# A two-layer trunk on one core: loads in layer 0's planner, column sums of the end in one group, paired stores, and a new order of layer 1's tiles

## The chip, the cores and the metric

The program runs on one NeuronCore of one Trainium2 chip. The metric is the device time of one execution in microseconds (us), the median over several runs. The profile is one execution of its own, recorded by the hardware profiler. Five engines work beside each other, each through its own queue in order: TensorE (PE, matrix products), VectorE (DVE), ScalarE (ACT), GpSimd (POOL) and SyncE (SP, which here only issues transfers).

## The reference

One step of a network with two layers on 640 tokens (128 of a prompt, 512 on a grid 64 columns wide) of 1024 features, all in f32. Cut to what matters:

```python
for i in range(2):                      # layer 0: conv branch, layer 1: SSD branch
    sh, sc, gt = split(silu(cond) @ ada_w[i] + ada_b[i], 3)
    h = rms_norm(y, norm_g[i]) * (1 + sc) + sh
    if i == 0:
        a, a_gate, z = split(h @ w_in + b_in, 3)               # 2048 features each
        v = depthwise_conv(a * sigmoid(a_gate), w_dw, b_dw)    # 31 taps, inside a grid row
        out = (silu(layer_norm(v)) * silu(z)) @ w_out
    else:
        z, xbc, dt_raw = split(h @ w_in)                       # 2048, 3072, 64
        xs, B, C = split(silu(depthwise_conv(xbc, w_conv, b_conv)))   # 5 taps
        dt = softplus(dt_raw + bias)                           # forward and backward
        yf = ssd_scan(xs, dt_f, B, C); yb = reversed ssd_scan  # chunks of 128 tokens
        out = rms_norm((yf + yb + d * xs) * silu(z)) @ w_out   # norm in 4 groups
    y = y + gt * out
return rms_norm(y, final_norm_g), final states
```

Prompt and grid have their own conditioning vectors and their own gate, scale and shift.

## The kernel before

**Layout.** Features lie on the 128 partitions, tokens along the row. The residual x is 8 tiles of 128 features x 640 tokens, the hidden width of 2048 is 16 tiles. The 640 tokens make two halves of 320 (`HN`), which fill the two banks of a PSUM tile.

**Products.** Each f32 product is made of three reduced-precision ones: a weight is split into a high part wh and a low part wl, the data into h_hi and h_lo, and wh·h_hi, wh·h_lo and wl·h_hi add up in PSUM. A projection of one 128-feature tile is 2 halves x 8 k-tiles x 3 = 48 matmuls of 320 columns (L619 in layer 0, `product`; L1277 in layer 1). For each weight tile, SP loads wf (L399), ScalarE casts wh (L418) and copies its negative to wl (L428), and GpSimd then issues a transfer of the same weights that adds onto wl (L429). In some steps of layer 0 and most of layer 1, VectorE subtracts instead (L1243). The tile wf has two buffers, wh and wl three.

**Layer 0.** For tile i, `a` and `g` are projected; ScalarE makes the sigmoid of g (L646), VectorE the product v (L659). The 31 taps on v are shared out: VectorE does most as multiply-adds in its own sum cva (L804); the widest-displaced `NPOOL[i]` taps are multiplied on ScalarE (tile tp, three buffers, L835) and added on GpSimd to cv (L876). VectorE's sum starts from a first term that ScalarE makes (L796), and is copied to cv by ScalarE (L811). Row crossings are put right in `seam_sums` (L848 to L870). `z` is projected and passed through silu (L675, which needs a table load on ScalarE), and the statistics of the layer norm come from column sums on TensorE, in the idle half of a bank, added up by VectorE (ssum, L730). The PSUM ring mm has two tiles: a projection can start when its tile's last reader is done. The modulation products of the coming steps ride on the same banks: `blocks` loads wa, four transfers of 256 KB for a block (L112), TensorE multiplies them ahead of a projection (L639), ScalarE copies the row (ada_row, L630), and TensorE turns it (L130), after which VectorE reads the values (L137).

**Layer 1.** 16 tiles x, 4 B, 4 C, 16 z, and 12 half-groups o of the output product are projected in an order written out by hand (names such as x21 are group and tile). The convolution of five taps on a projection is VectorE's (L1321) after ScalarE brings it out of PSUM (up, L1308). The time-step chain is a row of small steps on VectorE (L1867, L1870), whose results t, v, e and u TensorE turns to tokens (pt, L1934). The scan goes over groups and chunks: decays (L1618), chunk states pst (L1496) into VectorE's stn (L1524), from that po (L1559) and yo (L1563), then products py (L1627), gate and norm.

**The end.** The last output product (L1787) runs half 1 first, then half 0. Each of eight tiles gets its residual on VectorE (L1756), its square on ScalarE (L1761); GpSimd adds up the squares of the middle tiles. Column sums over the features are matmuls with ones (L184): a first group of two tiles of squares, copied to sm by VectorE (L1802), and a second group of the last tile, added to it (L1808). Then ScalarE's square root (L1809), the reciprocal (L1810) and a spread over the partitions on TensorE (L189). VectorE scales five tiles of a half straight from PSUM (L1815), GpSimd three from a copy of ScalarE's (L1823, L1826), and 16 stores of 128x320 leave from SP and ScalarE (L1830).

**The order of the work** is settled when the program is built. `Order` keeps a clock for each engine. Each chain of steps is a generator that yields operations with an engine and an estimated duration (`op`), keys to wait for (`key`) and buffers to take (`get`). `run` picks the operation that can start first, by the clocks, then by the priorities in PRIO0 and PRIO1 (lower first), and issues it. The emitted order is then fixed on every engine (`keep_order`), so planned durations and priorities decide the order and nothing else; at run time each engine waits at the head of its queue. PLAN0 and PLAN1 name the order in which weights are loaded and tiles projected. In `blocks` (L688) a block waits for the block two before it, and the first two have no condition. Transfers take only the clock of the engine that issues them.

Of the kernel before, what the change touches and what calls it, by code (L numbers as in the profile page):

```python
# [13 lines left out]
P = 128  # L14
# [35 lines left out]
def trunk(ctx: ExitStack, tc: tile.TileContext, a: dict):  # L50
# [193 lines left out]
    class Order:  # L244
# [63 lines left out]
        def run(self, until=None):  # L308
            while self.chains:
# [4 lines left out]
                for ch in self.chains:  # L314
# [3 lines left out]
                    for n, (eng, dur, fn, table) in enumerate(ways):  # L318
# [4 lines left out]
                        load = 1.28 if table and table != self.table else 0.0  # L323
# [6 lines left out]
                if table:  # L330
                    self.table = table
# [4 lines left out]
                ch[1] = t + dur + LATE.get(eng, 0.0)  # L336
                ch[5] = eng
# [6 lines left out]
    def op(eng, dur, fn, table=None):  # L344
        return "op", ((eng, dur, fn, table),)
# [4 lines left out]
    def key(*ks):  # L350
        return ("key",) + ks
# [26 lines left out]
    if True:  # L378
# [12 lines left out]
        def weights():  # L391
# [4 lines left out]
            for name, w in src:  # L396
                yield get("wf")
                wf = gp.tile([P, 1024], F32, tag="wf", bufs=2, name="wf")
                t = yield op(SP, 0.35, lambda: nc.sync.dma_start(out=wf, in_=w))  # L399
                start(split(name, wf, w), t)  # L400
# [186 lines left out]
    with tc.tile_pool(name="l0", bufs=1) as lp:  # L587
# [100 lines left out]
        def blocks():  # L688
            for n, (l, b) in enumerate(BLOCKS):
                if n > 1:  # L690
                    yield key(("ada", n - 2))
# [3 lines left out]
                t = yield op(SP, 1.8, lambda: blk.append(ada_load(l, b, cs, 2)))  # L695
# [146 lines left out]
        def seam_sums(i):  # L842
# [30 lines left out]
            for n, tap in enumerate(TAPS[:NPOOL[i]]):  # L873
                d, lo, hi = span_of(tap)
                yield key(("tp", i, n))
                t = yield op(PO, 1.28 + 0.0175 * (hi - lo - 49), lambda: G.tensor_add(out=rows64(cv[i], lo, hi), in0=rows64(cv[i], lo, hi), in1=sgs["tp", i, n][:, :, 0 : hi - lo]))  # L876
# [295 lines left out]
    if True:  # L1172
# [291 lines left out]
        def group(g):  # L1464
            yield key(("B", g), ("x", g, 3), *([("cols",)] if g == 0 else []))
# [286 lines left out]
        def last_residual(b, m, ps, ring):  # L1752
            tok = slice(b * HN, b * HN + HN)
            for cd, sl in SEGS:
                xv = x[m][:, tok][:, sl]
                t = yield op(VE, vec(sl.stop - sl.start) + 0.08, lambda: V.scalar_tensor_tensor(out=xv, in0=ps[:, sl], scalar=gain(1, m, cd), in1=xv, op0=ALU.mult, op1=ALU.add))  # L1756
            put(ring, t)
            nm, bufs = SQ[b]
            yield get(nm)
            sq = lp.tile([P, 512], F32, tag=nm, bufs=bufs, name="sq")[:, 0:HN] if b == 0 else lp.tile([P, HN], F32, tag=nm, bufs=bufs, name="sq")  # L1760
# [7 lines left out]
            post(("acc", b, m), t)  # L1768
            if m >= KD - REST[b]:
                t = yield op(ACT, 0.56, lambda: S.activation(out=x[m][:, tok], in_=x[m][:, tok], func=AF.Copy, scale=c("fg", m)))  # L1770
                post(("scaled", b, m), t)

        def last_products(b):
# [16 lines left out]
            post(("products", b), t)  # L1790

# [3 lines left out]
        def final(b):  # L1795
            tok = slice(b * HN, b * HN + HN)
            yield key(("acc", b, KD - 3), ("acc", b, KD - 2))
            yield get("b")
            ps = pq.tile([P, 512], F32, tag="b", bufs=3, name="rps")
            yield op(PE, 0.84, lambda: column_sums(ps[:, 384:387], accs[b][:2], PARTS))  # L1800
            sm, rc = (gp.tile([P, 3], F32, tag=nm, bufs=1, name=nm) for nm in ("sm", "rc"))
            yield op(VE, 0.16, lambda: V.tensor_copy(out=sm, in_=ps[:, 384:387]))  # L1802
# [314 lines left out]
```

## Time and profile before

| | us |
|---|---|
| median of 3 runs | 1088.61 (1088.28 to 1089.37) |
| profiled execution, its own time | 1088.08 |
| its span, first to last instruction | 1086.3 |
| TensorE busy | 1047.8 (96%) |
| VectorE, ScalarE, GpSimd busy | 795.1, 666.3, 456.4 |
| mean granted TensorE clock | 0.989 of full |

A row of the waits has the engine, the waiting operation with its line, what it waited for with its line, and the total, the count and the longest in us. A row of a timeline has the start, the duration from the first to the last of a row of like instructions, the engine, the line, the operation, output <- inputs, sizes and count; in brackets the idle time of the engine just before and what ended it. TensorE works through a pipeline: a matmul of 320 columns lasts about 0.31 us in a row, while the next starts 0.15 us after it. Numbers behind tile names are the program's own.

By place, TensorE's idle time in the span lies ahead of the first product and behind the last one (7.2 us at the start, 10.6 from the last product on), at a few places between, and hardly at all from 604 to 1070 us.

### The profile page before, as it was taken

How to read it: one execution, taken by the hardware profiler on the slowest of the kernel's cores; microseconds unless marked ns; L12 is line 12 of the kernel's file. 1: busy time of each engine (PE TensorE's matmuls, PEld its weight loads, DVE VectorE, ACT ScalarE, POOL GpSimd, SP SyncE). 2: the span in 40 equal slices, each digit the busy share in tenths (PEclk: the TensorE clock that was granted, in tenths of full speed). 3: DMA queues.
4: the chain of work that ended last, by engine and by line, in shares of the span. 5: the costliest groups of instructions: out<-in, count | busy, mean ns of one | idle time of the engine just before them, and what ended most of it. 6: DMA issues, size and time to landing. Idle time of an engine off the chain costs nothing. (4 is left out here: it accounts for less than half of the span.)

```text
span 1086.3 us, 19905 instructions
## 1 busy us (share of the span) xinstructions
PE 1047.8 (96%) x7888; PEld 976.3 (90%) x7888; DVE 795.1 (73%) x1188; ACT 666.3 (61%) x1093; POOL 456.4 (42%) x461
## 2 busy tenths in 40 slices
PE   6999999989999999999998999999999999999996
PEld 3898999989999999999998998988889988988895
DVE  2579999987999695103789597789777766776763
ACT  6457778878688686333576566585658353754442
POOL 0028989988599211111000145323531463364323
PEclk9999999999999999999999999999999999999997
DMA  9487787777755666676111635233341335343102
GB/s 362 181 227 190 205 214 180 183 206 209 189 124 135 138 144 152 150 163 130 59 63 66 160 87 136 69 108 98 107 117 64 102 107 127 91 105 107 40 20 97
DMA packets 86541, 146.94 MB, mean 135 GB/s; under 512 B 26928, under 2 KB 49840, under 8 KB 86448
## 3 DMA queue, kind: packets, MB, share of 16 engines
q1 hardware_dynamic: 77088, 113.91, 33.8%
q0 software_dynamic: 8640, 30.94, 16.3%
q8 instruction: 62, 1.02, 0.4%
q10 hardware_dynamic: 720, 0.82, 0.2%
q14 instruction: 31, 0.25, 0.1%
HBM read 140.73 MB, written 4.92 MB: 134 GB/s over the span
## 5 line engine op out<-in xcount | busy, mean ns | idle before, releaser
L804 DVE SCALAR_TENSOR_TENSOR cva<-v,cst,cva 128x620 f32<-128x620 f32 (+10 forms) x343 | 266.8, 823 | 16.3 <-ACT cva L796 11.8
L876 POOL TENSOR_TENSOR cv<-cv,tp 128x490 f32<-128x490 f32 (+5 forms) x137 | 174.9, 1276 | 10.1 <-ACT tp L835 1.2
L835 ACT ACTIVATE tp<-v,cst 128x490 f32<-128x490 f32 (+5 forms) x137 | 94.8, 719 | 41.6 <-POOL cv L876 41.2
L418 ACT CAST wh<-wf 128x1024 fp32r<-128x1024 f32 x63 | 65.9, 1045 | 67.9 <-PE o__5278 L155 29.9
L1239 ACT CAST wh<-wf 128x1024 fp32r<-128x1024 f32 x53 | 55.4, 1044 | 67.4 <-PE o L1277 25.6
L1277 PE MATMUL o<-yhl,wh 128*128 128x320 f32 x384 | 92.5, 328 | 0.0
L1277 PE MATMUL pz<-h_hi,wh 128*128 128x320 f32 x256 | 88.3, 345 | 1.3 <-ACT up L1308 1.3
L1243 DVE TENSOR_TENSOR wl<-wf,wh 128x1024 fp32r<-128x1024 f32 x48 | 66.2, 1379 | 31.5 <-ACT wh L1239 31.3
L1565 POOL TENSOR_TENSOR y<-y,yo 128x512 f32<-128x512 f32 x32 | 45.4, 1417 | 85.9 <-DVE yo L1563 82.6
L1277 PE MATMUL pz<-h_hi,wl 128*128 128x320 f32 x256 | 79.1, 309 | 0.0
L1277 PE MATMUL pz<-h_lo,wh 128*128 128x320 f32 x256 | 79.0, 309 | 0.0
L1277 PE MATMUL xs<-h_hi,wh 128*128 128x320 f32 x224 | 75.1, 335 | 0.0
L1321 DVE SCALAR_TENSOR_TENSOR xs<-up,cst,xs 128x642 f32<-128x642 f32 x64 | 66.1, 1032 | 7.4 <-PE ptx L1345 3.4
L1277 PEld LDWEIGHTS o<-yhl,wh 128*128 128x128 f32 x384 | 63.8, 188 | 7.5 <-issue 7.2
L1277 PE MATMUL xs<-h_lo,wh 128*128 128x320 f32 x224 | 69.9, 312 | 0.0
L1277 PE MATMUL xs<-h_hi,wl 128*128 128x320 f32 x224 | 69.9, 312 | 0.0
L429 POOL DMA_DIRECT2D wl<-w_in x43 | 37.4, 870 | 60.0 <-ACT wl L428 59.3
L428 ACT ACTIVATE wl<-wh 128x1024 fp32r<-128x1024 f32 x58 | 61.5, 1060 | 1.8
L1277 PE MATMUL o<-yhl,wl 128*128 128x320 f32 x192 | 59.4, 309 | 0.0
L1440 ACT ACTIVATE gf<-gf,cols 128x128 f32<-128x128 f32 x160 | 50.5, 391 | 8.5 <-DVE gf L1436 7.3
L1277 PEld LDWEIGHTS pz<-h_hi,wh 128*128 128x128 f32 x256 | 48.1, 188 | 7.2 <-issue 5.6
L1277 PEld LDWEIGHTS pz<-h_lo,wh 128*128 128x128 f32 x256 | 48.2, 188 | 3.8 <-issue 3.8
(842 smaller groups left out, 3379.3 us busy)
## 6 DMA issues: line engine op xcount, KB each, us to landing
wf<-w_in SPq DMA_DIRECT2D x48, 512.0 KB, 3.7
wl<-w_in POOLq DMA_DIRECT2D x43, 512.0 KB, 6.9
wa<-w_ada SPq DMA_DIRECT2D x64, 256.0 KB, 6.1
wf<-w_out SPq DMA_DIRECT2D x32, 512.0 KB, 3.7
wf<-w_xbc SPq DMA_DIRECT2D x24, 512.0 KB, 3.9
gf<-acd SPq DMA_DIRECT2D x40, 256.0 KB, 4.5
wa<-w_ada SPq DMA_DIRECT2D x16, 512.0 KB, 10.2
wf<-w_z SPq DMA_DIRECT2D x16, 512.0 KB, 3.7
```

What stands on the lines that cost most here:

```text
L418: t = yield op(ACT, 1.05, lambda: S.copy(out=wh, in_=wf))
L428: yield op(ACT, 1.06, lambda: S.activation(out=wl, in_=wh.bitcast(F32), func=AF.Copy, scale=-1.0))
L429: t = yield op(PD, 0.7, lambda: G.dma_start(out=wl, in_=src, accum_op=ALU.add))
L804: t = yield op(VE, 0.24 + 0.01 * (hi - lo), lambda: V.scalar_tensor_tensor(out=rows64(accs[i], lo, hi), in0=rows64(vs[i], lo + d, hi + d), ...
L835: t = yield op(ACT, 0.72, lambda: S.activation(out=tp[:, :, 0 : hi - lo], in_=rows64(vs[i], lo + d, hi + d), func=AF.Copy, scale=w_dw(i, t ...
L876: t = yield op(PO, 1.28 + 0.0175 * (hi - lo - 49), lambda: G.tensor_add(out=rows64(cv[i], lo, hi), in0=rows64(cv[i], lo, hi), in1=sgs["tp" ...
L1239: S.copy(out=cell["wh"], in_=cell["wf"])
L1243: e_.tensor_sub(out=cell["wl"], in0=cell["wf"], in1=cell["wh"].bitcast(F32))
L1277: T.matmul(ps[:, b, at_ : at_ + t1 - t0], lhsT=w_, rhs=t_[:, t0:t1], start=k == 0 and n == 0, stop=k == nk - 1 and n == 2)
L1321: t = yield op(VL, 0.89, lambda: V.scalar_tensor_tensor(out=acc, in0=u[:, d : d + PW], scalar=c("w_c", j * 5 + d), in1=acc, op0=ALU.mult, ...
L1440: t = yield op(ACT, 0.39, lambda: S.activation(out=gv[:, h_, :], in_=gv[:, h_, :], func=AF.Exp, bias=cols1[ch][:, o8 + h_ : o8 + h_ + 1]), ...
L1565: t = yield op(PO, 1.29, lambda: G.tensor_add(out=y, in0=y, in1=yo))
```

## The change

- `weights` and `blocks` in layer 0's planner: a load of SP or an adding load of GpSimd now moves a clock of the transfers (1.55 us for a wf, 3.1 for a block of wa or for an adding load), and its result is expected by that clock. The first two blocks wait for a weight's split; the rest as before. Some of GpSimd's and other estimates rise.
- PRIO0, PLAN0 and NPOOL: tiles 5 and 7 have 11 and 10 taps on GpSimd where they had 12; projection a15 stands behind z5 and z6.
- PRIO1 and PLAN1: every priority but a few, and the tile order of layer 1, are other numbers and another list. `group` waits for all four x tiles.
- The end: a group of column sums opens with a matmul of zeros (nil), adds nine matmuls in one PSUM group, and the square root reads PSUM; sm, its copy and its add are gone. The last tile's square of half 0 is made in two parts, the large one on ScalarE and the small one on VectorE. After half 1's products the planner's margin for TensorE is 0.3.
- x is one tile of 8 x 640 with views, and a store takes two feature tiles: 8 of 128x2x320.

The diff, cut to its core; of the two tile orders a part of a line stands here, and the priorities are left out:

```diff
-PLAN0 = "... g13 a13 g14 z4 a14 g15 a15 z5 z6 z7 ..."
-NPOOL = (12, 6, 12, 6, 12, 12, 8, 12, 2, 8, 9, 8, 12, 4, 6, 8)
+PLAN0 = "... g13 a13 g14 z4 a14 g15 z5 z6 a15 z7 ..."
+NPOOL = (12, 6, 12, 6, 12, 11, 8, 10, 2, 8, 9, 8, 12, 4, 6, 8)
...
-PLAN1 = "z00 x21 x03 b0 c0 x02 z01 x13 b1 x10 x11 z02 x12 z03 x20 ..."
+PLAN1 = "x03 z00 z01 x11 x02 b0 x10 c0 x13 z02 x31 c1 x21 x12 x20 ..."
...
-    x = []
-    for k in range(KD):
-        x.append(gp.tile([P, NT], F32, name=f"x{k}"))
+    xs_ = gp.tile([P, KD, NT], F32, name="x")
+    x = [xs_[:, k, :] for k in range(KD)]
+    nil = gp.tile([P, 3], F32, name="nil")
+    V.memset(nil, 0.0)
...
-                if table:
+                if table and eng == ACT:
                     self.table = table
...
+                if table and eng != ACT:
+                    self.clock[DM] = max(self.clock[DM], t + 0.3) + table
+                    ch[1] = max(ch[1], self.clock[DM] + (2.2 if eng == SP else -3.6))
...
     def op(eng, dur, fn, table=None):
-        return "op", ((eng, dur, fn, table),)
+        return "op", ((eng, dur, fn, table or (QUEUE if eng == PD else None)),)
+    QUEUE = 3.1
...
-                t = yield op(SP, 0.35, lambda: nc.sync.dma_start(out=wf, in_=w))
+                t = yield op(SP, 0.35, lambda: nc.sync.dma_start(out=wf, in_=w), 1.55)
...
         def blocks():
             for n, (l, b) in enumerate(BLOCKS):
-                if n > 1:
-                    yield key(("ada", n - 2))
+                yield key(("ada", n - 2) if n > 1 else ("w", tiles0[2 * n]))
...
-                t = yield op(SP, 1.8, lambda: blk.append(ada_load(l, b, cs, 2)))
+                t = yield op(SP, 1.8, lambda: blk.append(ada_load(l, b, cs, 2)), 3.1)
...
-            yield key(("B", g), ("x", g, 3), *([("cols",)] if g == 0 else []))
+            yield key(("B", g), *[("x", g, j) for j in range(4)], *([("cols",)] if g == 0 else []))
...
+            if m == KD - 1 and b == 0:
+                yield get(nm)
+                sq = square()
+                accs[b].append(sq)
+                small, large = sorted(SEGS, key=lambda z_: z_[1].stop - z_[1].start)
+                t = yield add(*large)
+                start(last_square(b, m, sq, tok, large[1]), t, f"residual{b}")
+                t = yield add(*small)
+                put(ring, t)
+                xv, sv = x[m][:, tok][:, small[1]], sq[:, small[1]]
+                t = yield op(VL, 0.2, lambda: V.tensor_mul(out=sv, in0=xv, in1=xv))
...
+            if b == 0:
+                run.lead = 0.3
...
-            yield key(("acc", b, KD - 3), ("acc", b, KD - 2))
+            yield key(("acc", b, KD - 3))
             yield get("b")
             ps = pq.tile([P, 512], F32, tag="b", bufs=3, name="rps")
-            yield op(PE, 0.84, lambda: column_sums(ps[:, 384:387], accs[b][:2], PARTS))
-            sm, rc = (gp.tile([P, 3], F32, tag=nm, bufs=1, name=nm) for nm in ("sm", "rc"))
-            yield op(VE, 0.16, lambda: V.tensor_copy(out=sm, in_=ps[:, 384:387]))
+            sums = ps[:, 384:387]
+
+            def add_up(n):
+                if n == 0:
+                    T.matmul(sums, lhsT=ones, rhs=nil, start=True, stop=False)
+                for i, (t0, nt) in enumerate(PARTS):
+                    T.matmul(sums[:, i : i + 1], lhsT=accs[b][n][:, t0 : t0 + nt], rhs=ones[:, 0:1], start=False, stop=n == 2 and i == 2)
+            yield op(PE, 0.92, lambda: add_up(0))
+            yield key(("acc", b, KD - 2))
+            yield op(PE, 0.69, lambda: add_up(1))
             yield key(("acc", b, KD - 1))
-            t = yield op(PE, 0.6, lambda: column_sums(ps[:, 388:391], accs[b][2:], PARTS))
+            t = yield op(PE, 0.69, lambda: add_up(2))
...
-            yield op(VE, 0.16, lambda: V.tensor_add(out=sm, in0=sm, in1=ps[:, 388:391]))
-            yield op(ACT, 0.26, lambda: S.activation(out=rc, in_=sm, func=AF.Sqrt, scale=1.0 / 1024, bias=epsb), "sqrt")
+            yield op(ACT, 0.26, lambda: S.activation(out=rc, in_=sums, func=AF.Sqrt, scale=1.0 / 1024, bias=epsb), "sqrt")
...
-                start(store(k, tok), t)
+                if k % 2:
+                    start(store(k, tok), t)
...
         def store(k, tok):
-            yield either((SP, 0.5, lambda: nc.sync.dma_start(out=a["o_y"][:, k, tok], in_=x[k][:, tok])), (ACT, 0.5, lambda: nc.scalar.dma_start(out=a["o_y"][:, k, tok], in_=x[k][:, tok])), bias=0.2)
+            two = slice(k - 1, k + 1)
+            yield either((SP, 0.6, lambda: nc.sync.dma_start(out=a["o_y"][:, two, tok], in_=xs_[:, two, tok])), (ACT, 0.6, lambda: nc.scalar.dma_start(out=a["o_y"][:, two, tok], in_=xs_[:, two, tok])), bias=0.2)
```

More of the change, by code (lines that the diff above doesn't have):

```diff
@@ L45 @@
-PLAN1 = "z00 x21 x03 b0 c0 x02 z01 x13 b1 x10 x11 z02 x12 z03 x20 c1 x23 x33 c2 x32 x22 z10 z11 o00 o01 z12 x30 z13 b2 o02 o03 z20 b3 o10 x31 z21 o11 z22 z23 c3 o12 z30 o13 z31 z32 o20 z33 o21 o22 o23"
+PRIO0 = {"firsts": 7, "ada_chain": 5, "modulation0": 3, "sums0": 4, "square0": 7, "first_split": -7, "conv": 3, "after_a": -5, "after_g": -7, "init": -7, "late_taps": 1, "late_adds": 3, "seam": 2, "copied": -6, "after_z": -7, "weights": 7, "split": -4, "row": 5, "square": -2, "filler": 5, "blocks": -1, "add_sums": -2, "stats": -5, "means": -3, "normalise": -4, "gate_z": 6, "late_block": -5, "residual": -3, "half_residual": -1, "root": -1, "modulation": 5, "split_h": 0, "scales": 6}
@@ L46 @@
+PLAN1 = "x03 z00 z01 x11 x02 b0 x10 c0 x13 z02 x31 c1 x21 x12 x20 x30 z03 b1 x22 x23 z10 x32 z11 o00 o01 c2 z12 z13 b2 o02 x33 o03 z20 z21 b3 z22 c3 z23 o10 o11 o12 o13 z30 z31 z32 o20 z33 o21 o22 o23"
 DONE0 = []
@@ L322, in run @@
                         t = max(self.clock[eng], ch[1] + wait, self.port if shared else -99.0)
-                        load = 1.28 if table and table != self.table else 0.0
+                        load = 1.28 if table and eng == ACT and table != self.table else 0.0
                         key = (t + 0.4 * load if len(ways) == 1 else t + dur - ways[0][1] + bias * n, ch[2], ch[3])
@@ L860, in products @@
                 G.tensor_tensor(out=pr, in0=win, in1=wv, op=ALU.mult)
-            t = yield op(PO, 1.04, products)
+            t = yield op(PO, 1.09, products)
             put("eb", t)
-            for a0, a1, n, d_ in ((0, 8, 7, 0.69), (0, 4, 4, 0.49), (0, 2, 2, 0.34), (0, 1, 1, 0.3)):
+            for a0, a1, n, d_ in ((0, 8, 7, 0.8), (0, 4, 4, 0.56), (0, 2, 2, 0.36), (0, 1, 1, 0.3)):
                 yield op(PO, d_, lambda: G.tensor_add(out=pr[:, :, a0 : a0 + n, :], in0=pr[:, :, a0 : a0 + n, :], in1=pr[:, :, a1 : a1 + n, :]))
@@ L1768, in last_residual, with scaled @@
             post(("acc", b, m), t)
+            yield from scaled(b, m, tok)
+        def scaled(b, m, tok):
             if m >= KD - REST[b]:
@@ L1771, in last_residual, with last_square @@
                 post(("scaled", b, m), t)
+        def last_square(b, m, sq, tok, sl):
+            yield op(ACT, 0.42, lambda: S.activation(out=sq[:, sl], in_=x[m][:, tok][:, sl], func=AF.Square))
+            t = yield key(("sqs", b, m))
+            post(("acc", b, m), t)
+            yield from scaled(b, m, tok)
         def last_products(b):
```

29 lines of the change are left out of this document (18 added, 11 removed).

## The prediction

> **What bounds the kernel now.** I read the busy line first, then the waits of TensorE, then each wait in the timelines, and the granted clock in the windows around them.
>
> ```profile
> span 1086.3 us, 19905 instructions
> PE 1047.8 (96%) x7888; PEld 976.3 (90%) x7888; DVE 795.1 (73%) x1188; ACT 666.3 (61%) x1093; POOL 456.4 (42%) x461
> ```
>
> TensorE (PE) is the bound: 1086.3 − 1047.8 = 38.5 us of idle is all that an order can win without removing work, and the change keeps TensorE's work (two tiny matmuls more). The waits of TensorE, with the total, the count and the longest:
>
> ```profile
> PE u__2798 L619 <- DVE ssum L730: 3.9, 1, 3.9
> PE pt L1934 <- DVE v L1870: 3.6, 1, 3.6
> ...
> PE u__907 L130 <- ACT ada_row L630: 2.2, 1, 2.2
> PE pz L1277 <- ACT up L1308: 1.3, 1, 1.3
> PE po L1559 <- DVE stn L1524: 1.3, 2, 1.0
> PE u__907 L619 <- DMA wl<-w_in: 1.2, 1, 1.2
> ...
> PE u__4007 L130 <- ACT ada_row L630: 0.4, 1, 0.4
> ```
>
> I call them A (u__907, wl, 1.2), B (u__907, ada_row, 2.2), C (u__2798, 3.9), D (u__4007, 0.4), E (pz, 1.3) and F (pt, 3.6). Two of them cost more than they last. Rows by stretch: length, busy times of PE, PEld, DVE, ACT and POOL, then the granted clock.
>
> ```profile
> 86.00:88.00 2.00, 0.58 (x13) 0.56 (x17) 1.93 (x3) 1.99 (x5) 1.87 (x2) 1.00 0.61 172
> 226.00:228.00 2.00, 1.17 (x5) 1.17 (x6) 1.71 (x3) 1.50 (x3) 1.92 (x2) 0.75 1.04 307
> 228.00:230.00 2.00, 2.00 (x9) 2.00 (x8) 2.00 (x4) 1.78 (x3) 1.76 (x5) 0.50 1.03 214
> 230.00:232.00 2.00, 2.00 (x14) 2.00 (x14) 1.97 (x3) 1.97 (x4) 0.00 (x0) 0.89 0.22 41
> 598.00:600.00 2.00, 1.90 (x11) 1.90 (x12) 1.96 (x5) 1.98 (x4) 0.00 (x0) 0.77 0.48 171
> ```
>
> After C the clock is short by 2 × (0.25 + 0.50 + 0.11) = 1.7 us; the stretch after F begins in the same way, so I charge 1.7 us there too. After B it stays at 1.00.
>
> **The change, part by part.**
>
> *A and B: the list of layer 0's loads.* SyncE (SP), first rows; wa are modulation weights, wf the input weights. Before:
>
> ```order
> L399 DMA wf<-w_in 128x1024 x3
> L112 DMA wa<-w_ada 128x512 x8
> L399 DMA wf<-w_in 128x1024 x4
> ```
>
> and after:
>
> ```order
> L404 DMA wf<-w_in 128x1024 x3
> L113 DMA wa<-w_ada 128x512 x4
> L404 DMA wf<-w_in 128x1024 x3
> L113 DMA wa<-w_ada 128x512 x4
> ```
>
> Four of the eight wa no longer stand ahead of the fourth wf. The condition that moves them is the planner's: it sets the order and adds no wait at run time. What that does to ScalarE (ACT), SP and VectorE (DVE):
>
> ```profile
> 54.13 3.65 SPq L112 DMA_DIRECT2D wa<-w_ada  x8
> 57.88 14.88 SPq L399 DMA_DIRECT2D wf<-w_in  x4
> 68.31 1.05 ACT L418 CAST wh<-wf 128x1024 fp32r<-128x1024 f32 x1 [8.81 <-DMA wf<-w_in]
> 71.26 4.34 DVE L804 SCALAR_TENSOR_TENSOR cva<-v,cst,cva 128x520 f32<-128x520 f32 x6 [5.48 <-ACT cva L796]
> 84.42 0.69 ACT L811 COPY cv<-cva 128x640 f32<-128x640 f32 x1 [5.61 <-DVE cva L804]
> ```
>
> ScalarE stands 8.81 us for that wf; the weight's low part (A) and the convolution's first term (DVE idle 5.48, then ScalarE 5.61 at 84.42, then ada_row, B) come late behind it. Four wa less are 1.8 us of issue (half of 3.65) and 1 MB of transfer. I expect wf 4.3 us earlier, more than A and B need: **−3.3**. At least 1.8 us earlier if only the issue counts, which still clears A: bounds −1.2 to −3.3. The moved wa come before the next wf but one, and no matmul waits for a wa there now; a second late wf would cost A again.
>
> *C: two taps fewer on GpSimd (POOL) in tile 7, one in tile 5.* The three adds go to VectorE.
>
> ```profile
> L876 POOL TENSOR_TENSOR cv<-cv,tp 128x540 f32<-128x540 f32 x12 | 16.2, 1352 | 0.6
> L804 DVE SCALAR_TENSOR_TENSOR cva<-v,cst,cva 128x630 f32<-128x630 f32 x32 | 28.0, 874 | 0.2
> 219.39 0.75 ACT L835 ACTIVATE tp<-v,cst 128x530 f32<-128x530 f32 x1 [1.48 <-POOL cv L876]
> 224.17 1.28 ACT L675 ACT_TABLE_LOAD   x1
> ```
>
> C is the PSUM bank of block z1, freed by VectorE's sum after ScalarE's silu (L675). The silu stands behind tap products (L835) that wait for GpSimd's buffers. GpSimd loses 3 × 1.35 = 4.1 us ahead of that point, VectorE gains 3 × 0.85 = 2.5. The silu should come 3 to 4 us earlier against TensorE, whose arrival is 3.3 earlier by A and B, as are the others' streams (GpSimd and VectorE wait there for the same wf). I leave 1.0 of C and no clock loss: −3.9 − 1.7 + 1.0 = **−4.6** (bounds −5.6 and −1). D goes with ScalarE's relief: **−0.4**.
>
> *The next bank.* VectorE is nearly full here.
>
> ```profile
> 88.00:222.00 134.00, 134.00 (x1225) 131.73 (x1215) 131.57 (x186) 107.24 (x165) 125.15 (x133) 1.00 0.75 190
> 261.25 0.89 DVE L659 SCALAR_TENSOR_TENSOR v<-u__3127,cst,sg 128x640 f32<-128x640 f32 x1 [3.79 <-ACT wh L418]
> 315.17 0.48 DVE L730 TENSOR_TENSOR ssum<-ssum,u__3719 128x320 f32<-128x320 f32 x1
> 316.11 1.08 PE L639 MATMUL u__3901<-wa,scz 128*32 128x128 f32 x32
> ```
>
> Block z4's bank is released at 315.65 and used at 316.11, 0.46 us later. TensorE comes 3.3 + 4.6 + 0.4 = 8.3 us earlier; VectorE 4.3 − 2.5 = 1.8, and 3.8 more if its idle time at 257.5 closes up. A new wait of 8.3 − 0.5 − 5.6 = **+2.2** (0 to 6.0). The granted clock after a wait of 2.2 us stayed at 1.00 (B). At the start it did not:
>
> ```profile
> PE ada L532 <- DMA wa<-w_ada: 3.1, 2, 2.5
> 22.00:24.00 2.00, 2.00 (x8) 1.69 (x8) 1.52 (x4) 0.39 (x1) 0.00 (x0) 0.55 1.05 418
> ```
>
> a longest wait of 2.5 us stood ahead of a clock of 0.55, so I charge 1.7 us from 2.5 on. The Trainium skill ("TensorE: Matmul & The Clock Gate", HAM oscillation) advises against idle gaps over about 3.4 us; by it, a wait of 3 us here would cost 3 and not 4.7. The start's row speaks for the lower limit, in a stretch that is sparse beside the gap as well.
>
> *E and F: layer 1's order found anew.* TensorE, before and after, at the first transposes pt of the time-step chain:
>
> ```order
> L1277 MATMUL xs<-h_hi,wl 128x320
> L1934 MATMUL pt<-cst,v 128x128 x3
> L1277 MATMUL xs<-h_hi,wh 128x320
> L1277 MATMUL xs<-h_lo,wh 128x320
> ```
>
> ```order
> L1281 MATMUL B<-h_hi,wl 128x320
> L1977 MATMUL pt<-cst,t 128x128 x3
> L1281 MATMUL B<-h_hi,wh 128x320
> L1281 MATMUL B<-h_lo,wh 128x320
> L1281 MATMUL B<-h_hi,wl 128x320
> L1977 MATMUL pt<-cst,v 128x128 x3
> ```
>
> On what moved: the first pt stands 19 matmuls later in the layer and needs t, not v. VectorE reaches its operand after 16 taps of the short convolution (L1321), not 20, and after eight weight subtractions (L1243), not seven.
>
> ```profile
> 584.97 3.66 DVE L1321 SCALAR_TENSOR_TENSOR xs<-up,cst,xs 128x642 f32<-128x642 f32 x4
> 595.05 1.22 DVE L1243 TENSOR_TENSOR wl<-wf,wh 128x1024 fp32r<-128x1024 f32 x1
> 592.53 0.31 PE L1277 MATMUL xs<-h_hi,wh 128*128 128x320 f32 x1
> 594.00 0.31 PE L1277 MATMUL xs<-h_lo,wh 128*128 128x320 f32 x1
> ```
>
> VectorE: −3.7 + 1.2 + 0.4 (two copies that now stand ahead) = 2.1 earlier. TensorE: 19 × 0.147 (ten matmuls from 592.53 to 594.00) = 2.8 later. Together 4.9 against 3.6: by the count F is gone. Taking each queued step with its own inputs instead, the convolutions that now stand ahead wait for projections that come later, and 1.9 remains. I take 1.0: −3.6 − 1.7 + 1.0 = **−4.3** (bounds −5.3 and 0). For E the evacuation (up) stands earlier on ScalarE, then the first weight's low part decides: **−0.4**.
>
> In the rest of layer 1 VectorE is far from full:
>
> ```profile
> 720.00:1070.00 350.00, 346.48 (x2367) 305.77 (x2366) 255.42 (x392) 190.13 (x355) 138.63 (x109) 1.00 0.31 87
> ```
>
> TensorE idles 3.5 us of 350. The new order has the same work and as many hand-offs. Of the 24 state hand-offs (pst to stn to po, the wait of 1.3 above) the least covered has 1.7 us of products in between (rows times pitch), where the least was 2.2. **+0.5** (−2 to +6).
>
> The planner's costs, its DMA clock and its priorities act through the orders alone; six table loads fewer on ScalarE (1.28 each) and the two small copies of VectorE lie beside TensorE's work.
>
> *The end.* The rows behind the last product hold half 1's last column sums and its spread (L184, L189) as well as half 0's, which ends last:
>
> ```profile
> 1069.99 2.06 PE L184 MATMUL rps<-ones,sq 128*128 128x1 f32 x18
> 1072.45 0.83 PE L184 MATMUL rps<-ones,sq 128*128 128x1 f32 x6 [0.40 <-DVE sm L1802]
> 1073.14 1.31 PE L189 MATMUL rps<-cst,rc 128*128 128x128 f32 x6
> 1075.17 1.65 PE L189 MATMUL rps<-cst,rc 128*128 128x128 f32 x6 [0.72 <-DVE rc L1810]
> 1075.06 7.36 SPq L1830 DMA_DIRECT2D o_y<-x  x11
> ...
> 1078.00:1084.00 6.00, 0.00 (x0) 0.00 (x0) 2.32 (x5) 0.00 (x0) 2.51 (x4) 0.50 0.96 349
> ```
>
> After, TensorE has half 1's inside the products:
>
> ```order
> L1838 MATMUL rps<-nil,ones 128x3
> L1840 MATMUL rps<-ones,sq 128x1 x9
> L1819 MATMUL o_11364<-yhl,wh 128x320 x2
> L1819 MATMUL o_11364<-yhl,wl 128x320
> ```
>
> The spread stands a little later among them. That adds to the dense stream one nil, three sums (two records each, 2.06 / 18 a record) and one spread: 0.2 + 0.7 + 1.3 = 2.3 us. Behind the last product go half 1's spread (1.31), its three sums (0.7), the wait for the copied sums (0.40) and the slow clock of the last spread (1.65 − 1.31 = 0.3): 2.7. SP then has four stores behind the last half's scaling, not eleven of both at 7.36 / 11 = 0.67 each; I count 1.0 for that. The last store is of 320 KB, and 160 KB more take 0.5 us at the rate here. −2.7 − 1.0 + 0.5 + 2.3 = **−0.9** (−2 to +0.5). The Trainium skill ("DMA: Bandwidth & Descriptors", Anatomy of one DMA) gives a fixed 2.0 us and bytes over 436 GB/s; by it the larger last store costs 0.4 (my estimate from that page) and the end brings −1.0.
>
> **Sum**: −3.3 − 4.6 − 0.4 + 2.2 − 4.3 − 0.4 + 0.5 − 0.9 = −11.2. The profiled run took 1088.08 (span 1086.3 and 1.8 around it): 1076.9, and 1077.4 against the median of 1088.61.
>
> **Rivals.**
> 1. *VectorE becomes layer 0's bound.* Its idle time at 257.5 does not close, z4 waits 6.0 and loses 1.7 of clock: 5.5 more, 1082.9. For it: 131.57 of 134 busy and three adds more. Against: what it waited for there, a weight cast on ScalarE, moves with TensorE.
> 2. *The waits go altogether.* C, F and the new one at z4 cost nothing, 4.2 less: 1073.2. For it: the count at F. Against: 0.46 us of slack at z4.
> 3. *C and F only move.* GpSimd's buffers still decide C, and t is as late as v was; both keep their length and clock loss: 8.9 more, 1086.3. Against: GpSimd loses 4.1 us of work before C.
> 4. *Slower: the state hand-off.* Each of the 24 hand-offs pst to stn to po sets TensorE waiting, since VectorE's queue has conversions ahead of stn. It decides from (11.2 + 2.2) / 24 = 0.56 us each; at 0.7 each 16.8 us, 1094.2. For it: the lesser cover. Against: only two wait now, 1.3 us in all.
>
> **How the numbers follow.** The forecast 0.53, rival 1 0.17, rival 2 0.12, rival 3 0.10, rival 4 0.08. About 0.2%, 2.2 us, can be told from no change here. Faster: forecast, rivals 1 and 2, and half of rival 3: 0.87; same 0.05; slower 0.08. The range from 1070.0 (rival 2 with −2 in the rest of layer 1 is 1070.7) to 1086.3 leaves out rival 4, half of rival 3 and a little below: some 0.16. The three bounds that are widest, z4's 6.0, F's 0 and the rest's +6, lie inside it one at a time.
>
> **What would show it.** Right: no wait of about 1 and 2 us at 77 and 85; z1's bank wait near 1 us with the clock at 1.00 around 225; a new wait of about 2 us on ssum near 310; pt waiting about 1 us; half 1's rps among the products and an end of about 13 us behind the last one, not 16. The prediction is wrong if waits beyond 2.5 us appear in layer 1, if the clock still drops after C or F, or if the new z4 wait exceeds 4 us.

## The result and the profile after

The changed kernel takes 1072.57 us (median of 4 runs, 1069.97 to 1073.52), the kernel before 1088.99 (4 runs). The ratio is 0.9844, with a 95% interval of 0.9824 to 0.9864: 16.4 us or 1.6% faster. The forecast was 1077.4, in a range of 1070.0 to 1086.3. The profiled execution took 1072.78, with a span of 1071.0.

First the busy times and then TensorE's waits of the changed kernel, in the order and units of the prediction's rows:

```profile
span 1071.0 us, 19887 instructions
PE 1043.6 (97%) x7892; PEld 973.2 (91%) x7892; DVE 798.2 (75%) x1191; ACT 655.2 (61%) x1081; POOL 456.3 (43%) x459
```

```profile
PE rps L198 <- ACT rms_sq L505: 7.4, 2, 7.2
PE ada L537 <- DMA wa<-w_ada: 5.2, 4, 3.5
PE pt L1977 <- DVE t L1967: 2.0, 1, 2.0
PE xs L1281 <- ACT up L1312: 0.8, 1, 0.8
PE rps L1840 <- ACT sq L1784: 0.7, 1, 0.7
```

A, B, C and D are gone and nothing took their place in layer 0; F is 2.0 instead of 3.6, E 0.8 instead of 1.3. TensorE's busy time fell by 4.2 us with all but the same matmuls. Of that 1.3 lie in the start, ahead of A's place, and 2.3 in the rest of layer 0 (1.7 of them are the clock behind C). Behind the last product it is 2.5 less, since sums and a spread moved from there into the products, where they add 1.9. Layer 1 loses 1.7 us of clock in both kernels: before behind F, after behind half 1's sums. Where the 15.3 us of the span went, by the start times of the same products in both timelines:

| place | before | after | gained up to here |
|---|---|---|---|
| first projection of layer 0 | 22.17 | 23.55 | −1.4 |
| projection ahead of A's and B's place | 76.61 | 77.35 | −0.7 |
| projection behind it | 87.74 | 84.60 | 3.1 |
| second projection behind z1's bank | 236.51 | 227.83 | 8.7 |
| end of layer 0's products | 530.97 | 521.74 | 9.2 |
| end of the last product | 1070.15 | 1058.82 | 11.3 |
| end of the span | 1086.3 | 1071.0 | 15.3 |

So 3.9 us come from A and B, 5.5 from C with its clock, 0.6 from D and the next bank, 2.1 from layer 1, 3.9 from the end. The first row is the start's wait for wa (longest 2.5 us before, 3.5 here); in the twelve kernels below the first projection starts between 21.8 and 23.6 us, whatever was changed.

The rows that answer to A and B: SP's list, the cast that waited 8.81 us, and the first term of the convolution.

```profile
54.88 1.75 SPq L113 DMA_DIRECT2D wa<-w_ada  x4
56.74 8.00 SPq L404 DMA_DIRECT2D wf<-w_in  x3
```

```profile
63.33 1.05 ACT L423 CAST wh<-wf 128x1024 fp32r<-128x1024 f32 x1 [3.08 <-DMA wf<-w_in]
64.41 1.06 ACT L433 ACTIVATE wl<-wh 128x1024 fp32r<-128x1024 f32 x1
65.38 0.87 ACT L800 ACTIVATE cva<-v,cst 128x640 f32<-128x640 f32 x1
```

The fourth wf is cast at 63.33, not 68.31: 5.0 us earlier, where I had put 4.3. The rows that answer to z1's and z4's banks, ScalarE's silu first:

```profile
216.87 1.28 ACT L680 ACT_TABLE_LOAD   x1
218.16 0.79 ACT L680 ACTIVATE sz<-u__2583,cst 128x640 f32<-128x640 f32 x1
```

```profile
252.56 0.88 DVE L664 SCALAR_TENSOR_TENSOR v<-u__3108,cst,sg 128x640 f32<-128x640 f32 x1 [1.41 <-PE u__3108 L198]
306.73 0.48 DVE L734 TENSOR_TENSOR ssum<-ssum,u__3707 128x320 f32<-128x320 f32 x1
```

The silu ends 7.3 us earlier (218.95 against 226.25). z4's bank is released at 307.2 and used at 307.42: a slack of 0.2 where it was 0.46, and no wait. Then the end:

```profile
1039.38 1.48 PE L1840 MATMUL rps<-ones,sq 128*128 128x1 f32 x12
1041.58 0.83 PE L1840 MATMUL rps<-ones,sq 128*128 128x1 f32 x6 [0.73 <-ACT sq L1784]
1045.28 1.22 PE L190 MATMUL rps<-cst,rc 128*128 128x128 f32 x6
```

```profile
1058.80 2.15 PE L1840 MATMUL rps<-ones,sq 128*128 128x1 f32 x18
1061.51 0.93 PE L190 MATMUL rps<-cst,rc 128*128 128x128 f32 x6 [0.56 <-DVE rc L1850]
```

```profile
1063.57 1.68 POOL L1867 TENSOR_TENSOR x<-x,rb 128x320 f32<-128x320 f32 x2 [6.02 <-ACT rb L1864]
```

```profile
1064.10 2.38 SPq L1873 DMA_DIRECT2D o_y<-x  x4
```

Half 1's sums and spread stand among the products, and behind the last product there are 12.2 us, not 16.1 (three other executions of the old end under layer 1's old order have 17.1). This gain has a price: among the products TensorE's busy time is 1.9 us longer, it waits 0.73 for a square between the sums, and in this execution a stretch at half clock follows them, which loses another 1.7 (length, busy times of PE, PEld, DVE, ACT and POOL, then the clock):

```profile
1039.26:1042.67 3.41, 2.68 (x24) 2.60 (x24) 2.20 (x6) 2.93 (x7) 0.00 (x0) 1.00 0.00 0
1042.67:1046.09 3.42, 3.42 (x15) 3.42 (x15) 0.74 (x3) 0.04 (x1) 0.00 (x0) 0.50 0.00 0
```

So 3.9 us won behind the last product stand against 2.6, and in this execution 4.3, among the products.

### The profile page after: what moved, and what is told of

The parts are those of the page before. It is cut to its first block, busy times and chain, and to the rows that moved or that the text cites. A ratio compares the mean times of both kernels' runs of the same rounds, so it can differ in the third digit from the quotient of the medians.

```text
span 1071.0 us, 19887 instructions
## 1 busy us (share of the span) xinstructions
PE 1043.6 (97%) x7892; PEld 973.2 (91%) x7892; DVE 798.2 (75%) x1191; ACT 655.2 (61%) x1081; POOL 456.3 (43%) x459
## 4 chain that ended last, share of the span: by engine, by line
PE 85%; DVE 7%; ACT 4%; DMA 2%; issue 1%; SPq 0%; POOL 0%; DVEq 0%; ACTq 0%
PE pz L1281 8%; PE o L1281 8%; PE xs L1281 4%; PE po L1563 3%; PE o L1819 3%; PE pst L1500 2%; DVE xs L1325 2%; PE C L1281 2%; PE B L1281 2%; PE py L1631 2%; PE o__4958 L156 1%; PE o__5267 L156 1%; PE o__5258 L156 1%; PE o__5245 L156 1%; PE o__5238 L156 1%; PE o__4948 L156 1%
## 5 line engine op out<-in xcount | busy, mean ns | idle before, releaser
L808 DVE SCALAR_TENSOR_TENSOR cva<-v,cst,cva 128x550 f32<-128x550 f32 (+12 forms) x346 | 270.1, 822 | 11.7 <-ACT cva L800 6.6
L839 ACT ACTIVATE tp<-v,cst 128x490 f32<-128x490 f32 (+5 forms) x134 | 92.4, 718 | 36.8 <-POOL cv L880 36.3
L1247 DVE TENSOR_TENSOR wl<-wf,wh 128x1024 fp32r<-128x1024 f32 x47 | 63.8, 1358 | 17.6 <-ACT wh L1243 17.5
L1325 DVE SCALAR_TENSOR_TENSOR xs<-up,cst,xs 128x642 f32<-128x642 f32 x64 | 62.6, 981 | 4.6 <-PE rms L1685 2.1
L1438 POOL TENSOR_TENSOR gb<-gb,cols 128x512 f32<-128x512 f32 x20 | 24.0, 1198 | 79.2 <-DVE xs L1325 65.1
```

The costliest lines, as they stand in the source:

```text
L808: t = yield op(VE, 0.24 + 0.01 * (hi - lo), lambda: V.scalar_tensor_tensor(out=rows64(accs[i], lo, hi), in0=rows64(vs[i], lo + d, hi + d), ...
L839: t = yield op(ACT, 0.72, lambda: S.activation(out=tp[:, :, 0 : hi - lo], in_=rows64(vs[i], lo + d, hi + d), func=AF.Copy, scale=w_dw(i, t ...
L1247: e_.tensor_sub(out=cell["wl"], in0=cell["wf"], in1=cell["wh"].bitcast(F32))
L1325: t = yield op(VL, 0.89, lambda: V.scalar_tensor_tensor(out=acc, in0=u[:, d : d + PW], scalar=c("w_c", j * 5 + d), in1=acc, op0=ALU.mult, ...
```

## The experiments

Each kernel was timed against the kernel before on the same chip; "before" in the table is that of the same rounds.

| kernel | us, median (range) | before | ratio, 95% interval |
|---|---|---|---|
| list only | 1084.61 (1082.73–1086.45) | 1088.82 | 0.9952 (0.9933–0.9972) |
| taps only | 1089.85 (1087.96–1090.93) | 1088.82 | 1.0003 (0.9992–1.0014) |
| end only | 1088.01 (1085.56–1091.75) | 1088.82 | 0.9991 (0.9977–1.0005) |
| layer 1 only | 1083.04 (1080.64–1083.17) | 1088.82 | 0.9931 (0.9911–0.9951) |
| estimates only | 1084.87 (1083.54–1086.67) | 1089.32 | 0.9960 (0.9945–0.9975) |
| all, old taps | 1075.48 (1073.60–1076.37) | 1089.32 | 0.9871 (0.9855–0.9886) |
| all, old estimates | 1077.49 (1076.05–1079.21) | 1089.32 | 0.9889 (0.9870–0.9908) |
| all, old end | 1070.87 (1070.14–1073.74) | 1089.32 | 0.9836 (0.9818–0.9853) |
| the change again | 1073.09 (1071.93–1073.86) | 1088.24 | 0.9856 (0.9842–0.9870) |
| later turns | 1078.57 (1075.06–1080.98) | 1088.24 | 0.9906 (0.9889–0.9922) |
| later turns, old end | 1080.67 (1079.20–1082.56) | 1088.24 | 0.9926 (0.9913–0.9939) |
| all, old list | 1076.69 (1076.21–1081.02) | 1088.24 | 0.9899 (0.9884–0.9915) |

**List only.** The kernel before with the transfer clock and the condition of the first blocks.

```diff
-                if n > 1:
-                    yield key(("ada", n - 2))
+                yield key(("ada", n - 2) if n > 1 else ("w", tiles0[2 * n]))
+                if table and eng != ACT:
+                    self.clock[DM] = max(self.clock[DM], t + 0.3) + table
```

> The kernel before with the new list of layer 0's loads alone (transfer clock and the condition of the first two blocks; taps, projections, layer 1 and end as before). Theory: A and B (1.2 and 2.2 us) come from the four wa ahead of the fourth wf and go; C does not come from them but from GpSimd's taps, so TensorE's wait on z1's bank stays, between 2.5 and 4.5 us, with its loss of clock. Time 3 to 4 us shorter than before. Rival (C is a late effect of the same wf): C falls under 1 us as well, and the time is 8 to 9.5 us shorter.

```profile
PE pt L1937 <- DVE v L1873: 3.6, 1, 3.6
...
PE u__2798 L623 <- DVE ssum L733: 2.4, 1, 2.4
```

A and B are gone, C stays at 2.4 us (and two small waits, 0.3 and 0.5, behind it), 4.2 us shorter. C is just under the 2.5 expected, and it brings no loss of clock in this execution. The list explains A and B, and not C.

**Taps only.** `NPOOL` with 11 and 10 alone.

```diff
-NPOOL = (12, 6, 12, 6, 12, 12, 8, 12, 2, 8, 9, 8, 12, 4, 6, 8)
+NPOOL = (12, 6, 12, 6, 12, 11, 8, 10, 2, 8, 9, 8, 12, 4, 6, 8)
```

> The kernel before with 11 and 10 taps on GpSimd in tiles 5 and 7 alone. Theory: A and B stay (1.2 and 2.2 us), the wait on z1's bank falls from 3.9 to under 1.5 us and the clock near 228 us stays at 1.00: 4 to 5.5 us shorter. Rival (C follows from the late wf): C stays at over 2.5 us and the time falls by less than 2 us.

```profile
PE u__2795 L619 <- DVE ssum L730: 4.9, 1, 4.9
```

```profile
221.17 0.75 ACT L835 ACTIVATE tp<-v,cst 128x530 f32<-128x530 f32 x1 [1.71 <-POOL cv L876]
221.82 1.03 ACT L418 CAST wh<-wf 128x1024 fp32r<-128x1024 f32 x1
222.88 1.06 ACT L428 ACTIVATE wl<-wh 128x1024 fp32r<-128x1024 f32 x1
223.84 1.29 ACT L835 ACTIVATE tp<-v,cst 128x490 f32<-128x490 f32 x2
225.19 0.74 ACT L704 ACTIVATE sq<-cv 128x640 f32<-128x640 f32 x1
225.83 0.70 ACT L835 ACTIVATE tp<-v,cst 128x490 f32<-128x490 f32 x1
226.53 1.28 ACT L675 ACT_TABLE_LOAD   x1
```

My theory fell: with fewer taps on GpSimd the wait is 4.9 us, and the time unchanged. The three profiled executions with an unchanged layer 0 (before, the new end alone, layer 1 alone) have 3.9, 2.3 and 1.6 us there, so the wait varies by itself, but it has not become shorter. The timeline shows why. The planner's estimates put GpSimd's four seam adds of a tile at 1.82 us, where a row of the kernel before has 2.14:

```profile
207.48 2.14 POOL L864 TENSOR_TENSOR seam<-seam 128x210 f32<-128x210 f32 x4
```

It takes GpSimd's adds to be done too early, and so puts tap products of the next tiles ahead of z1's silu, and with the new taps tile 7's square as well, which waits for GpSimd's last add there. Counted in the order, 80 tap products stand ahead of that silu in the kernel before, with the new list alone and with the new taps alone, but 78 in the changed kernel. With the new taps alone three products of the next tiles have thus taken the place of the three that were removed. Three buffers between ScalarE and GpSimd make that two adds of GpSimd, 2.6 us. The part of the change that does it is the raised estimates for GpSimd. The next three runs test this, the three estimates together; which of them decides was not tried apart.

**Estimates only.** The three estimates alone.

```diff
-            t = yield op(PO, 1.04, products)
+            t = yield op(PO, 1.09, products)
-            for a0, a1, n, d_ in ((0, 8, 7, 0.69), (0, 4, 4, 0.49), (0, 2, 2, 0.34), (0, 1, 1, 0.3)):
+            for a0, a1, n, d_ in ((0, 8, 7, 0.8), (0, 4, 4, 0.56), (0, 2, 2, 0.36), (0, 1, 1, 0.3)):
-                t = yield op(PO, 1.28 + 0.0175 * (hi - lo - 49), ...
+                t = yield op(PO, 1.3 + 0.019 * (hi - lo - 49), ...
```

> The kernel before with the planner's raised estimates for GpSimd alone (products, adds, taps; GpSimd keeps 12 taps in tiles 5 and 7, the list is the old one). In this order z1's silu stands behind 78 tap products on ScalarE, not 80, which needs two adds of GpSimd less (2.6 us by their rows). New theory (the place of the silu decides C, not the number of taps): A and B stay, the wait on z1's bank falls by about 2.6 us from what kernels with the old place show (1.6 to 3.9), to between 0 and 1.3, and the time by 2 to 5 us. Rival (fewer taps on GpSimd are what helps, as the prediction had it): the wait stays between 1.6 and 3.9 us and the time within 1 us of before.

```profile
PE u__907 L130 <- ACT ada_row L630: 1.7, 1, 1.7
PE u__907 L619 <- DMA wl<-w_in: 1.7, 1, 1.7
...
PE u__2792 L619 <- DVE ssum L730: 1.2, 1, 1.2
```

A and B stay, C falls to 1.2 us with no loss of clock (a wait of 0.9 us for ada_row comes up some 20 us behind it), 4.4 us shorter.

**All, old taps**: the changed kernel with the old `NPOOL`.

> The changed kernel with 12 taps on GpSimd in tiles 5 and 7 again, all else as changed; the silu of z1 still stands behind 78 tap products. New theory: TensorE's wait on z1's bank stays under 0.6 us and the time within 1.5 us of the changed kernel (1071 to 1074.5). Rival of the prediction (the taps): a wait of 2 us or more with a loss of clock comes back, 4 us or more longer (over 1076.5).

No wait on z1's bank, as the new theory has it. The time is 2.4 to 2.9 us above the two timings of the changed kernel, more than expected, though the intervals overlap: a wait for ada_row some 20 us later (0.9 us) stands there that the changed kernel doesn't have, and layer 1 has one stretch more at half clock (1.7 us) in this execution. So the taps may be worth something, but not at C.

```profile
PE u__2898 L131 <- ACT ada_row L635: 0.9, 1, 0.9
```

**All, old estimates**: the changed kernel with the three old estimates.

> The changed kernel with the old estimates for GpSimd and its 11 and 10 taps. Here z1's silu stands behind 80 tap products and a square that waits for tile 7's last add on GpSimd. New theory: the wait on z1's bank is back at 2.4 to 5 us with a loss of clock of 1 to 1.7, time 3.5 to 6.5 us above the changed kernel (1076 to 1079). Rival (the taps): no wait over 1 us, time within 1.5 us of the changed kernel.

```profile
PE u__2790 L624 <- DVE ssum L734: 4.0, 1, 4.0
```

C is back with its loss of clock, and 4.4 to 4.9 us with it. Put in or taken out, C follows the estimates. In all 14 traces the wait goes with the place of the silu: with 80 tap products ahead of it the wait is 1.6 to 4.9 us (six executions), with 78 it is 1.2 once and otherwise absent (eight). The silu was not moved by itself.

**End only, layer 1 only, and all with the old end.** The first has the new code of the end, the second `PRIO1`, `PLAN1` and `group`, the third the change without the code of the end.

```diff
+            if b == 0:
+                run.lead = 0.3
-            yield op(PE, 0.84, lambda: column_sums(ps[:, 384:387], accs[b][:2], PARTS))
+            yield op(PE, 0.92, lambda: add_up(0))
```

> The kernel before with the new end alone (column sums in one group, split square, paired stores), layer 1's priorities as before. In this order half 1's last sums and both spreads stand behind the last product, as before. Theory of the prediction (the gain at the end comes from half 1's sums and spread having moved into the products): without that move the end behind the last product falls by 1 to 2 us only, from 16.1 to about 14.5 to 15, and the time by 1 to 2 us. Rival (the removed copy, add and half of the stores make the gain): the end falls by 3 to 4 us, to 12 to 13.

> The kernel before with layer 1's priorities and tile order alone (layer 0 and the code of the end as before). Theory: E falls to under 1 us, F from 3.6 to about 2 us and without loss of clock, layer 1's small gaps fall by 1 to 2 us, and half 1's sums and spread move into the products, which shortens the end behind the last product by about 2.5 us and lengthens the products by 2.3: 4.5 to 6.5 us shorter in all. Rival (F only looks shorter because layer 0 ends in another state): F stays over 3 us, and the time falls by less than 3 us.

> The changed kernel with the old code of the end: two groups of column sums with a copy and an add, 16 single stores, the square of the last tile in one part. Half 1's sums and spread still stand among the products. Theory: the end behind the last product grows from 12.2 to about 13.7 us, as with layer 1's order alone, and the time by 1 to 2 us (1073.5 to 1074.6). Rival (the new code brings nothing by itself, as it did under the old order): the end stays within 0.5 us of 12.2.

From the last product to the end of the span: 16.1 us before, 15.9 with the new code alone, 13.7 with layer 1's tables alone, 12.7 with the change but for the end's code, 12.2 with all. The place of half 1's sums and spread, which layer 1's new tables set (`PRIO1`, `PLAN1` and `group` together), makes most of the gain; the code by itself 0.2 to 0.7 us there. With the new end alone neither the theory (14.5 to 15) nor the rival (12 to 13) came about; for the old end the rival held. (The step from 13.7 to 12.7 goes with the clock, which no run has apart: TensorE is at half clock from 1.9 us behind the last product in the one and from 4.1 us in the other. With the new code and half clock from 2.0 us, as in all with the old taps, it is 12.9.) Against the changed kernel the old end is not slower (1070.87 against 1072.57 and 1073.09), while with the later turns, below, it was slower (1080.67 against 1078.57); the ranges overlap, so whether the new code helps or hurts as a whole stays open. With layer 1 alone the time is 5.8 us shorter, as expected; with the new end alone it is 0.8, and the interval of its ratio holds 1. With layer 1 alone the waits are as expected too, with pt at 2.4 us:

```profile
PE pt L1934 <- DVE t L1924: 2.4, 1, 2.4
...
PE xs L1277 <- ACT up L1308: 0.8, 1, 0.8
```

**The change again, later turns, later turns with the old end.** F's 2.0 us were left. The planner takes t for ready too early, so the transposes of t and v were planned 2.5 us later:

```diff
-        def turn_columns(n, z):
+        def turn_columns(n, z, lag=0.0):
+            post(("turn", n), run.clock[VE] + lag)
+            yield key(("turn", n))
```

> The changed kernel once more, as the measure for the runs beside it. Theory of the clock, from the runs so far (fixed stretches of 3.41 us; half clock for one stretch after one in which TensorE was idle for 60% or more, none at 56% or less): the wait on pt is 2.05 us again, and the clock falls after it only if it lies so that one stretch holds 2.05 us of it. Time 1070 to 1073.5. Rival (a wait of a given length always or never costs clock): the clock stays at 1.00 after pt, as in the first profile of this kernel.

> The changed kernel, with the transposes of t and v (pt) planned 2.5 us after VectorE's clock, which puts them 18 matmuls later. Theory: the wait on pt (2.05 us) goes, with the share of the clock loss that it brought; no other wait grows by more than 0.5 us; 1.5 to 3.5 us shorter than the changed kernel beside it. Rival (the columns that hang on pt are needed at once): a wait of 1.5 to 2.5 us comes up in the first group of the scan and the time stays within 0.7 us.

> As the kernel with the later transposes, with the old code of the end (two groups of sums, copy and add, 16 single stores). Theory from the earlier run (the new code of the end brings nothing that can be measured once half 1's sums stand among the products): within 1 us of the kernel with later transposes and the new end. Rival (the new end brings 1 to 2 us): 1 to 2 us longer.

In the change again the clock fell after pt, as the theory has it (last section). With the later turns the wait on pt went and the kernel became 5.5 us slower, and with the old end 2.1 more, the size that the rival had. The waits of later turns, whose profiled execution is the fastest of its six and 1.9 us slower than that of the change again:

```profile
PE ptx L1349 <- ACT xs L1327: 1.8, 1, 1.8
PE o L1281 <- DVE x L1413: 1.7, 1, 1.7
PE xs L1281 <- DVE x L1413: 1.3, 1, 1.3
PE pz L1281 <- ACT up L1312: 0.9, 1, 0.9
```

```profile
593.17 0.74 ACT L1327 ACTIVATE xs<-xs 128x642 f32<-128x642 f32 x1 [2.83 <-DVE xs L1325]
```

1.8 us return 4 us later, for an x tile whose convolution VectorE ends late: VectorE is behind as a whole there, whichever of its results TensorE asks for first. The rest is a worse order of the planner's further on, in places that the edit doesn't touch: TensorE's idle time between layer 0's last product and the last product of all rises from 4.9 to 9.4 us. My theory was wrong and the rival was near, though it had the wrong place. None of the versions tried is shown to beat the change.

**All, old list**: the change with the old list of loads.

> The changed kernel with the old list of layer 0's loads (no transfer clock, first blocks without condition: eight wa ahead of the fourth wf). Theory: A and B are back with 1 and 2 to 2.8 us, z1's wait stays under 1 us; 3 to 5 us longer than the changed kernel beside it, more by 1.7 or 3.4 if B takes a stretch's 60%. Rival (the raised estimates for GpSimd spread the loads as well): no wait at 77 to 85 us, within 1 us.

```profile
PE u__902 L131 <- ACT ada_row L631: 2.0, 1, 2.0
PE u__902 L620 <- DMA wl<-w_in: 1.6, 1, 1.6
```

A and B are back, 3.6 us longer than the change beside it; z1's bank has no wait.

Each tried alone on the kernel before, the list gives 4.2 us, the estimates 4.4, layer 1's tables 5.8, the end 0.8 and the taps −1.0 (within the noise), together 14.2 of the 15.2 to 16.4 us of the whole. `PRIO0` and `PLAN0` were not tried apart.

## Why the prediction was right, and where not

The time lay in the range, 4.8 us below the forecast. Between the −11.2 of the sum and the −15.3 of the spans, the next bank and D make 2.4, C 0.9, the end 0.7, A and B 0.6 and layer 1 0.2; the start took 0.7 back.

- **A and B** (forecast −3.3, measured −3.9): right in cause and size. List only and all with the old list show it from both sides.
- **C** (−4.6, measured −5.5 with its clock in this execution, 4.4 to 4.9 by the medians of the runs with the estimates put in or taken out): the gain was right and its cause wrong. The step "GpSimd loses 3 × 1.35 = 4.1 us ahead of that point" credited the taps; the raised estimates, of which the prediction said only that they "act through the orders alone", move the silu ahead of two tap products. Behind the new taps alone ScalarE still has 80 products ahead of the silu, so that GpSimd has no less to add there. Taps only gave no gain; estimates only gave C's.
- **The next bank** (+2.2, measured 0): the step that failed, and the largest error of the sum. It moved VectorE by "4.3 − 2.5 = 1.8, and 3.8 more if its idle time at 257.5 closes up". VectorE was free for v of that projection at 257.46 before and at 251.15 after (start less the idle time of its row), 6.3 earlier: it also lost 1.8 us of waiting in C itself, and the whole 5.5 at 71.26 (with the three adds that makes 4.8; 1.5 stay unassigned). It then waits for TensorE in both kernels (3.79 and 1.41 us). The row before names a weight cast, and the prediction took it so, but v starts 0.14 and 0.13 us behind the bank's last column sums, and after it starts in the middle of such a cast. So from there on the two move together (VectorE 8.4, TensorE 8.7 us earlier at z4), and the slack at z4 stays near what it was (0.46, then 0.2).
- **F** (−4.3, measured −3.3: 1.6 of wait and 1.7 of clock in this execution): of the two workings, the one that took each queued step with its own inputs gave 1.9 and the trace 2.0; the mere count of VectorE's work gave none. The middle that I took was the worse choice. The 1.7 of clock are chance: in the change again the clock fell after pt, one of the prediction's own signs of being wrong.
- **The rest of layer 1** (E −0.4, rest +0.5, sums among the products +2.3, with F −1.9 in all): measured −2.1 in all, by errors that cancel. The sums and the spread cost 4.3 in this execution (1.9 busy, 0.7 of waiting, 1.7 of clock), not 2.3. E gave 0.5, and TensorE's other waits, of which po, rms and pst were the longest, fell by 2.6 where the prediction had a loss of 0.5.
- **The end** behind the last product (−3.2, measured −3.9): right, and layer 1 only shows that the place does it. What the prediction gave to fewer stores (1.0) is not seen with the new code alone: 0.2. With the sums among the products the forecast was −0.9 in all; it became +0.4 in this execution, and −1.3 without the stretch at half clock. The figures of the Trainium skill ("DMA: Bandwidth & Descriptors", Anatomy of one DMA) that the prediction set beside its 0.5 for the larger last store are given there for transfers that GpSimd issues; no run here has the larger store alone.
- **Clock.** "I charge 1.7 us from 2.5 on" is wrong as a rule: see below. At F before it held by chance of place; C's 3.9 us leave hardly a place where no stretch takes 58% of idle time (1.95 us on either side are 57%).

The rivals: 2 (the waits go altogether) came nearest, since C and the new wait at z4 cost nothing, with F left. Rival 1 did not occur, since VectorE still idles at 252. Rivals 3 and 4 did not occur; the state hand-off's wait fell from 1.3 to 0.4 us.

## What to carry to other kernels

A planner that thinks one engine too fast puts work that waits for it ahead of work that others wait for: correct the estimate before you move work off that engine. Count a shift between two engines only up to the next place where one waits for the other in both kernels; behind it they move together. And count a gain of ordering where it is made, with its price: the same code at the end brought 0.2 us in one order and stood beside a gain of 3.9 in another, and the order that made the 3.9 cost 2.6 to 4.3 among the products.

## What the runs showed of the hardware

The clock after a gap of TensorE depends on where the gap lies. In every trace the changes of the granted clock lie on a raster of 3.41 us, which lies elsewhere in the span in each execution. A stretch of that raster at full clock in which TensorE idled for 58% or more was followed by one at half clock; at 30 to 56% it was not, but for one stretch that held sums of the end. The same wait of 2.05 us on pt, in two executions of the changed kernel, first as one that fell across two stretches, then as one that fell into one stretch (rows of successive stretches; PE's busy time first, the clock behind the engines):

```profile
585.29:588.70 3.41, 2.76 (x19) 2.49 (x17) 3.28 (x8) 0.82 (x2) 0.00 (x0) 1.00 0.07 15
588.70:592.11 3.41, 2.02 (x15) 2.01 (x16) 3.38 (x5) 2.95 (x5) 0.00 (x0) 1.00 0.39 121
592.11:595.52 3.41, 3.41 (x28) 3.30 (x26) 2.22 (x5) 1.22 (x3) 0.00 (x0) 1.00 0.33 90
```

```profile
588.46:591.88 3.42, 1.35 (x11) 1.09 (x10) 3.38 (x7) 2.74 (x4) 0.00 (x0) 1.00 0.18 12
591.88:595.29 3.41, 3.41 (x15) 3.37 (x15) 3.31 (x5) 1.06 (x3) 0.00 (x0) 0.50 0.63 202
```

With estimates only, F's whole 3.6 us cost no clock, since they were split 1.7 and 1.9 (in the rows, the stretch's length less PE's busy time):

```profile
588.99:592.41 3.42, 1.68 (x12) 1.42 (x10) 3.35 (x4) 1.88 (x3) 0.00 (x0) 1.00 0.00 0
592.41:595.82 3.41, 1.50 (x11) 1.51 (x12) 3.27 (x8) 3.36 (x7) 0.00 (x0) 1.00 0.50 154
595.82:599.23 3.41, 3.41 (x26) 3.40 (x25) 3.34 (x5) 1.54 (x3) 0.00 (x0) 1.00 0.73 48
```

With the new end alone the same 3.6 us were followed by two stretches at half clock, 3.4 us lost. Between 40 and 1056 us the 14 profiled executions have 14 stretches with an idle share of 0.58 to 1.00, all followed by half clock, and 36 with 0.30 to 0.56. Of these 34 were followed by full clock; one came at half clock itself, and one was full of the end's sums. Three of the 14 stretches at half clock were followed by a second one, at idle shares of 0.17, 0.24 and 0.55; what decides that stays open. The end's sums, matmuls of one column, seem to count for little: the changed kernel goes to half clock behind half 1's sums (1042.7 to 1046.1 us) at an idle share of 0.21. It doesn't always: in the change again it stays at full clock at the same share, and of the nine executions with these sums among the products five go to half clock behind them. The Trainium skill ("TensorE: Matmul & The Clock Gate", Part 1) has a free-running window of 3413 ns, with which this agrees; its advice to keep gaps under about 3.4 us (HAM oscillation) is too lenient here: 2.05 us sufficed. So a gap between 2.0 and 3.6 us had a price that changed from run to run, 0 to 3.4 us. This and the clock behind the sums can make part of the 3.6 us between the fastest and the slowest of the changed kernel's first four runs, of which one was traced; the start can make another, since the two traced executions of this kernel are 1.2 us apart already ahead of A's place (77.35 and 78.60).
